# Attention with stacked rotary queries, pre-scaled queries and query projections between the heads

## The chip, the cores and the metric

The kernel runs on one core of one Trainium2 chip. The metric is the time of one execution in microseconds of device time. Engines are named as in the profile: PE is TensorE (PEld its weight loads), DVE is VectorE, ACT is ScalarE, POOL is GpSimd, SP is SyncE, which here only issues DMAs. Matrix products go from on-chip memory into eight PSUM banks of 128 x 512 float32; ACT and DVE read them from there.

## The reference

A two-layer trunk: layer 0 mixes tokens with an mLSTM, layer 1 with multi-head latent attention, and each is followed by a gated convolutional FFN and LayerNorms. 256 latent tokens attend to 256 context tokens and themselves. What the change touches is the attention of layer 1 (8 heads, 128 dimensions without and 64 with rotary position, values of 128):

```python
def _mla_q(h, w_dq, q_norm, w_uq, ang):
    q = (_rms_norm(h @ w_dq, q_norm) @ w_uq).reshape(B, T, A_HEADS, A_DNOPE + A_DROPE)
    q_nope, q_rope = jnp.split(q, [A_DNOPE], axis=-1)
    return jnp.concatenate([q_nope, _axial_rope(q_rope, ang[0][:, None], ang[1][:, None])], -1)

def _mla_kv(h, w_dkv, kv_norm, w_ukv, ang):
    ckv, k_rope = jnp.split(h @ w_dkv, [A_KVLORA], axis=-1)
    if ang is not None:
        k_rope = _axial_rope(k_rope, ang[0], ang[1])
    kv = (_rms_norm(ckv, kv_norm) @ w_ukv).reshape(B, T, A_HEADS, A_DNOPE + A_DV)
    k_nope, v = jnp.split(kv, [A_DNOPE], axis=-1)
    k = jnp.concatenate([k_nope, broadcast(k_rope over the heads)], -1)
    return k, v

def _attend(q, k, v):
    s = jnp.einsum("bqhd,bkhd->bhqk", q, k).astype(jnp.float32) * ((A_DNOPE + A_DROPE) ** -0.5)
    p = jax.nn.softmax(s, axis=-1).astype(v.dtype)
    return jnp.einsum("bhqk,bkhd->bqhd", p, v)
```

The rotary key is one for all heads. The result goes through `w_out`, then gate, residual and LayerNorm, then the FFN of layer 1.

## The kernel before

Numbers are float32, but matrix products run on a reduced type (float32r). Each operand is therefore split into a high part (a cast on ACT) and a low part (source minus high part, on DVE), and a product is three passes into one accumulator: high x high, high x low, low x high (`mm3`, L310 to L314). A split of a PSUM tile is `split` (L316 to L318); a weight of 128 x 1024 is split in `Stream._split` (ACT L256, DVE L257).

Weights come in one fixed order (`_plan`) through `Stream`. SP loads them into a ring of three `raw` buffers (L239); a load waits until the split that used its buffer three places before has ended. `use(key)` splits ahead of use, up to eight places and not past `self.limit`; `pump(n)` sets that limit to place n of the order and splits up to it. Split weights lie in three buffers `w`, and some ("wide" ones) in the large pool `u` of 31 buffers, as `wu`. Small tiles (`s2`) come from a pool of 13.

Background work is written as generators: `self.bg` holds them, `tick()` runs one step, `drain()` runs all the rest. The engines' order is set by a scheduler when the kernel is built, from the program's order and its own estimate of times; on the chip each engine runs its instructions in that order and waits on semaphores.

The attention of layer 1, in the order of the program:

- `mla_ctx`: the context's `dkv` product (512 context and latent columns share `ckT0`, `ckT1` and `krT`), root-mean-square norm, transposes (`dkv_T`). `krT` holds the rotary key transposed, copied twice, on rows 0 to 63 and 64 to 127; high part in index 0, low part in index 1.
- `mla_kv`, `ukn(0)`, `uv(0)`: keys and values of the context. Meanwhile `after0` ends the LayerNorm of the FFN before. A last piece of it, `ln_x`, is put off (`late`): four broadcast loads of gain and bias on POOL's queue (L932), then eight DVE operations (L1032, L1033) and four stores to `x2d` (L1034), which the residual of the attention reads later.
- `mla(hl)`: `dkv` and `dq` products of the latent tokens, norms, `dkv_T`, `ukn(1)`, transposes of the normed queries (`cqT`), `uv(1)` (24 passes into `v`), the rotary queries `qr` (weights `uqr`) with their rotation on DVE (`rope_rows`), then the other queries `qn` of all eight heads (weights `uqn`, with a `tick()` after each head, which is where the steps of `ln_x` are run), then the rotary queries transposed and split: `qrT` holds two heads per 128 rows, 64 rows each. `drain()` follows.
- The heads, a pipeline in which the scores of head h are followed by `attend` of head h - 2. `scores(h)`: per tile of 128 queries three passes of `qn` with `kn` on 128 rows and three of `qrT` with `krT` on 64 rows, row maximum (L1337), times minus the scale (L1338), exponential with scale, bias and sum (L1340), reciprocal and scaling (L1341, L1342). `trans`: eight transposes of P, split. `attend`: twelve passes with `v`, split into `oT`.
- `pump(ao + h)` stands ahead of heads 1 to 7; `ao` is the place of the first `aout` weight, so `aout` 0 to 6 are split in the heads.
- `aout`, the product with `w_out`: weight k belongs to head k, and `aout` 0 is used before the last head's `attend`. Then LayerNorm (`after0`: `ln_rows`, `ln_T`) while the first six `fin1` weights of the FFN are split, then the FFN.

Of the kernel before, what the change touches and what calls it, by code (L numbers as in the profile page):

```python
# [7 lines left out]
F32 = mybir.dt.float32  # L8
F32R = mybir.dt.float32r
I32 = mybir.dt.int32  # L10
AF = mybir.ActivationFunctionType
ALU = mybir.AluOpType
AX = mybir.AxisListType
# [12 lines left out]
H1 = 8  # L26
DN, DR, DV = 128, 64, 128
# [4 lines left out]
NB, NRAW, NU = 3, 3, 31  # L32
# [251 lines left out]
class K:  # L284
# [863 lines left out]
    def dkv_mm(self, hT, wd):  # L1148
        rows = [self.ps("dkv"), self.ps("dkv")]
        for k in range(8):  # L1150
            w = wd[k // 3]
            c = slice((k % 3) * 320, (k % 3 + 1) * 320)
            hi, lo = hT(k)
            for t in range(2):
                ts = slice(t * 128, (t + 1) * 128)
                self.mm3(rows[t][:, :320], (hi[:, ts], lo[:, ts]), (w[0][:, c], w[1][:, c]), k == 0, k == 7)
        return rows
# [17 lines left out]
    def dkv_T(self, out, t0):  # L1175

        nc = self.nc
        g = self.smc("kvg")
        cs = slice(t0 * 128, t0 * 128 + 256)
        for k in range(3):  # L1180
            pt = self.ps("ckT")
            for t in range(2):
                nc.tensor.transpose(pt[:, t * 128:(t + 1) * 128], out[t][:, k * 128:(k + 1) * 128], self.ident)
            p = pt[:, 0:256]
            if k < 2:
                u = self.ckT[k]
                nc.scalar.activation(u[:, 0, cs], p, AF.Copy, scale=g[:, k:k + 1])
                nc.vector.scalar_tensor_tensor(u[:, 1, cs], p, g[:, k:k + 1], u[:, 0, cs],
                                               op0=ALU.mult, op1=ALU.subtract)
            else:  # L1190
                self.split(self.krT[:, 0, cs], self.krT[:, 1, cs], p)

    def ukn(self, g):

# [26 lines left out]
    def mla_ctx(self, hc):  # L1221
        self.wd = [self.st.use(("dkv", 0, c), hold=True) for c in range(3)]
        self.ckT = [self.u("ckT0"), self.u("ckT1")]
        self.krT = self.u("krT")
        self.dkv_T(self.dkv_rows(self.dkv_mm(hc, self.wd), 0), 0)

    def rope_load(self):
# [13 lines left out]
    def mla(self, hl):  # L1241
# [2 lines left out]
        rows = self.dkv_rows(self.dkv_mm(hl, self.wd), 2)  # L1244
        self.wd = None
        st.unhold("dkv")
        pss = [self.ps("dq0"), self.ps("dq1")]
        for c in range(4):
            w = st.use(("dq", 0, c))
            for kk in range(2):  # L1250
                k = 2 * c + kk
                hi, lo = hl(k)
                cs = slice(kk * 384, (kk + 1) * 384)
                for t in range(2):
                    ts = slice(t * 128, (t + 1) * 128)
                    self.mm3(pss[t][:, :384], (hi[:, ts], lo[:, ts]), (w[0][:, cs], w[1][:, cs]), k == 0, k == 7)
# [9 lines left out]
        for k in range(3):  # L1266
# [5 lines left out]
            nc.vector.scalar_tensor_tensor(u[:, 1], pt[:, 0:256], g[:, k:k + 1], u[:, 0],  # L1272
                                           op0=ALU.mult, op1=ALU.subtract)
            cqT.append(u)
        self.uv(1)
        self.ckT = self.wk = self.wv = None
        kn, v = self.kn, self.v1
        pss = [self.ps("qr0"), self.ps("qr1")]
        for c in range(2):
            w = st.use(("uqr", 0, c))  # L1280
            for kk in range(2 - c):
                k = 2 * c + kk
                cs = slice(kk * 512, (kk + 1) * 512)
                for t in range(2):
                    ts = slice(t * 128, (t + 1) * 128)
                    self.mm3(pss[t], (cqT[k][:, 0, ts], cqT[k][:, 1, ts]), (w[0][:, cs], w[1][:, cs]),
                             k == 0, k == 2)
        qr = []
        for t in range(2):
            r = self.s2("qr")  # L1290
            self.rope_rows(r, pss[t], t, 512)
            qr.append(r)
        self.ropet = None
        qn = []
        ws = {}
        for h in range(H1):
            if h % 2 == 0:
                ps = self.ps("qn")
            hs = slice((h % 2) * 256, (h % 2 + 1) * 256)
            for k in range(3):  # L1300
                b = h * 3 + k
                if b % 8 == 0:
                    ws = st.use(("uqn", 0, b // 8))
                c = slice((b % 8) * 128, (b % 8 + 1) * 128)
                self.mm3(ps[:, hs], (ws[0][:, c], ws[1][:, c]), (cqT[k][:, 0], cqT[k][:, 1]), k == 0, k == 2)
            if h % 2:
                u = self.u("qn")
                self.split(u[:, 0], u[:, 1], ps)
                qn.append(u)
            self.tick()  # L1310
        qrT = []
        for i in range(2):
            pt = self.ps("qrT")
            for j in range(2):
                b = 2 * i + j
                for t in range(2):
                    nc.tensor.transpose(pt[:, j * 256 + t * 128:j * 256 + (t + 1) * 128],
                                        qr[t][:, b * 128:(b + 1) * 128], self.ident)
            u = self.u("qrT")
            self.split(u[:, 0], u[:, 1], pt)  # L1320
            qrT.append(u)
        self.drain()
        scale = float((DN + DR) ** -0.5)
        krT = self.krT

        def scores(h):
            Ps = []
            for t in range(2):
                ps = self.ps("s1")
                c = slice((h % 2) * 256 + t * 128, (h % 2) * 256 + (t + 1) * 128)  # L1330
                self.mm3(ps, (qn[h // 2][:, 0, c], qn[h // 2][:, 1, c]), (kn[h][:, 0], kn[h][:, 1]), True, False)
                b = h // 2
                r = slice((h % 2) * 64, (h % 2 + 1) * 64)
                c = slice((b % 2) * 256 + t * 128, (b % 2) * 256 + (t + 1) * 128)
                self.mm3(ps, (qrT[b // 2][r, 0, c], qrT[b // 2][r, 1, c]), (krT[r, 0], krT[r, 1]), False, True)
                mx, sm = self.tiny(1, "mx"), self.tiny(1, "sm1")
                nc.vector.tensor_reduce(mx, ps, axis=AX.X, op=ALU.max)  # L1337
                nc.vector.tensor_scalar(mx, mx, -scale, None, op0=ALU.mult)  # L1338
                P = self.s2("P1")
                nc.scalar.activation(P, ps, AF.Exp, bias=mx, scale=scale, accum_out=sm)  # L1340
                nc.vector.reciprocal(sm, sm)  # L1341
                nc.vector.tensor_scalar(P, P, sm, None, op0=ALU.mult)  # L1342
                Ps.append(P)
            return Ps
# [29 lines left out]

        ao = st.nu
        Ps, PTs = {}, {}
        for h in range(H1 + 1):
            if 1 <= h < H1:
                st.pump(ao + h)
            if h >= 2:  # L1380
                PTs[h - 2] = trans(h - 2, Ps.pop(h - 2))
            if h < H1:
                Ps[h] = scores(h)
            if h >= 2:
                attend(h - 2, PTs.pop(h - 2))
        yield oT
# [179 lines left out]
```

## Time and profile before

| | us |
|---|---|
| median of 3 runs (lowest, highest) | 1441.57 (1440.91, 1443.89) |
| the profiled execution | 1443.13 |
| its span, from the first to the last instruction | 1441.4 |
| PE busy in it | 1408.5 (98%) |
| DVE busy | 981.0 (68%) |
| ACT busy | 639.7 (44%) |
| POOL busy | 100.0 (7%) |
| mean granted clock of TensorE | 0.991 |

Durations and starts below are from the profiled execution, in microseconds from the start of its span. [...] The granted clock is the share of full speed that TensorE was given. The attention of layer 1 lies between about 1075 (the context's `dkv`) and 1240 (the end of `aout`), its heads between 1159.6 and 1217. A wait is put down to what came last before it ended.

### The profile page before, as it was taken

Reading aid. Unit: us, or ns where it says so; the run is one execution under the profiler, and the core shown is the slowest. Engines: PE = TensorE matmul, PEld = TensorE weight load, DVE = VectorE, ACT = ScalarE, POOL = GpSimd, SP = SyncE. Lnnn points to the kernel's source line nnn. Section 1 sums busy time; section 2 is a strip of 40 time slices with the busy share of each in tenths; the row PEclk is TensorE's granted clock in tenths of the full one; section 3 lists DMA queues with packets and bytes.
Section 4 is the critical chain, followed back from the end, with each engine's and each line's share of the span. In section 5 each row is a group of like instructions: output and inputs, shape, how many; then the busy total and the mean of one; then the engine's idle time right before and its main releaser. Section 6 shows DMA issues by size and latency. Waiting matters only on the chain.

```text
span 1441.4 us, 18835 instructions
## 1 busy us (share of the span) xinstructions
PE 1408.5 (98%) x7094; PEld 1178.2 (82%) x7094; DVE 981.0 (68%) x1451; ACT 639.7 (44%) x968; POOL 100.0 (7%) x185
## 2 busy tenths in 40 slices
PE   7999999999999999999999999999999989999997
PEld 3788888888878888878888888888888967899986
DVE  6796879985676676666787544444658677777756
ACT  6554232224333354464643333334455545555542
POOL 0011010003001010210001000000000001000000
PEclk9999999999999999999999999999999989999999
DMA  9475776777774645645645333345564334357763
GB/s 338 167 237 193 241 249 208 257 237 275 238 225 152 203 162 160 192 174 171 213 129 174 89 116 123 119 124 181 184 187 145 126 108 133 135 177 214 226 202 103
DMA packets 82828, 262.71 MB, mean 182 GB/s; under 512 B 11352, under 2 KB 19752, under 8 KB 82736
## 3 DMA queue, kind: packets, MB, share of 16 engines
q1 hardware_dynamic: 68304, 214.82, 46.6%
q0 software_dynamic: 14144, 46.17, 9.4%
q8 instruction: 55, 0.90, 0.3%
q10 hardware_dynamic: 288, 0.52, 0.1%
q14 instruction: 37, 0.30, 0.1%
HBM read 243.56 MB, written 17.91 MB: 181 GB/s over the span
## 4 chain that ended last, share of the span: by engine, by line
PE 67%; issue 18%; DMA 6%; DVE 4%; ACT 2%; POOL 2%; SPq 0%; DVEq 0%; POOLq 0%; ACTq 0%
PE fin L314 8%; PE fin L312 8%; PE fin L313 8%; PE y L313 5%; PE y L314 5%; PE y L312 5%; PE qk L312 4%; PE qk L314 4%; PE qk L313 4%; DMA raw<-in_ws 3%; DMA ar<-in_ada_w 2%; PE up L312 1%; PE up L314 1%; PE up L313 1%; PE s L312 1%
## 5 line engine op out<-in xcount | busy, mean ns | idle before, releaser
L257 DVE TENSOR_TENSOR w<-raw,w 128x1024 fp32r<-128x1024 f32 (+2 forms) x267 | 324.0, 1213 | 242.7 <-ACT w L256 242.1
L256 ACT CAST w<-raw 128x1024 fp32r<-128x1024 f32 (+2 forms) x267 | 278.8, 1045 | 437.3 <-PE tok L314 149.5
L314 PE MATMUL fin<-h,w 128*128 128x256 f32 (+1 forms) x696 | 231.6, 333 | 0.5 <-DVE w L257 0.5
L313 PE MATMUL fin<-h,w 128*128 128x256 f32 (+1 forms) x696 | 231.7, 333 | 0.0
L312 PE MATMUL fin<-h,w 128*128 128x256 f32 (+1 forms) x696 | 231.5, 334 | 0.0
L437 DVE SCALAR_TENSOR_TENSOR acc<-ar,cond,acc 128x1024 f32<-128x1024 f32 x112 | 140.6, 1279 | 36.2 <-DMA ar<-in_ada_w 35.9
L314 PEld LDWEIGHTS fin<-h,w 128*128 128x128 f32 x696 | 132.2, 190 | 13.8 <-DVE w L257 0.9
L313 PEld LDWEIGHTS fin<-h,w 128*128 128x128 f32 x696 | 132.2, 190 | 13.0 <-DVE h L1017 0.2
L312 PEld LDWEIGHTS fin<-h,w 128*128 128x128 f32 x696 | 131.9, 190 | 12.8
L314 PE MATMUL qk<-xc,w 128*128 128x512 f32 x256 | 100.2, 391 | 2.0 <-DVE w L257 2.0
L312 PE MATMUL qk<-xc,w 128*128 128x512 f32 x256 | 101.1, 395 | 0.0
L312 PE MATMUL tok<-w,xm 128*128 128x512 f32 x256 | 100.4, 392 | 0.0
L313 PE MATMUL qk<-xc,w 128*128 128x512 f32 x256 | 99.9, 390 | 0.0
L314 PE MATMUL tok<-w,xm 128*128 128x512 f32 x256 | 99.7, 389 | 0.0
L313 PE MATMUL tok<-w,xm 128*128 128x512 f32 x256 | 99.6, 389 | 0.0
L312 PE MATMUL y<-w,act 128*128 128x512 f32 (+1 forms) x212 | 80.4, 379 | 0.0
L313 PE MATMUL y<-w,act 128*128 128x512 f32 (+1 forms) x212 | 80.1, 378 | 0.0
L314 PE MATMUL y<-w,act 128*128 128x512 f32 (+1 forms) x212 | 80.1, 378 | 0.0
L314 PEld LDWEIGHTS qk<-xc,w 128*128 128x128 f32 x256 | 48.1, 188 | 12.7 <-DVE w L257 2.7
L312 PEld LDWEIGHTS tok<-w,xm 128*128 128x128 f32 x256 | 48.0, 188 | 10.3
L257 DVE TENSOR_TENSOR wu<-raw,wu 128x1024 fp32r<-128x1024 f32 x36 | 43.9, 1222 | 18.4 <-ACT wu L256 18.0
L314 PEld LDWEIGHTS tok<-w,xm 128*128 128x128 f32 x256 | 48.1, 188 | 10.1
(357 smaller groups left out, 2771.7 us busy)
## 6 DMA issues: line engine op xcount, KB each, us to landing
raw<-in_ws SPq DMA_DIRECT2D x300, 512.0 KB, 3.8
ar<-in_ada_w SPq DMA_DIRECT2D x80, 512.0 KB, 4.6
adaw<-in_ada_w SPq DMA_DIRECT2D x32, 256.0 KB, 6.0
xcd<-cv POOLq DMA_DIRECT2D x16, 256.0 KB, 3.3
od<-o POOLq DMA_DIRECT2D x16, 256.0 KB, 4.0
vd<-v POOLq DMA_DIRECT2D x16, 256.0 KB, 4.0
xcr<-xcd POOLq DMA_DIRECT2D x16, 256.0 KB, 6.3
vr<-vd POOLq DMA_DIRECT2D x16, 256.0 KB, 4.1
```

Source lines behind the costliest of these rows:

```text
L256: k.nc.scalar.copy(h[:, :cols], raw[:, :cols])
L257: k.nc.vector.tensor_sub(l[:, :cols], raw[:, :cols], h[:, :cols])
L312: mm(out, w[0], x[0], start=start, stop=False)
L313: mm(out, w[0], x[1], start=False, stop=False)
L314: mm(out, w[1], x[0], start=False, stop=stop)
L437: nc.vector.scalar_tensor_tensor(acc[j], w, s, acc[j], op0=ALU.mult, op1=ALU.add)
```

## The change

Five things change.

1. The rotary queries are split before they are transposed: `qrs` holds, per head, 64 high and 64 low columns, already times the scale. Transposed, one head fills 128 rows, the high part on rows 0 to 63 and the low part below. `krT` is the high key on both halves in index 0, and in index 1 the low key on rows 0 to 63 and zeros below (a memset in `mla_ctx`). Two passes then give the same three products: (high and low) x high, high x low. There are four transposed tiles instead of two, each with four transposes and one copy on ACT, and they lie in the pool `s2`.
2. The scale is put into the queries `qn` and `qrs` (`activation` with a scale, `scalar_tensor_tensor`), so the row maximum is negated by the reduction itself, L1338 goes, and the exponential has scale 1.
3. The queries of heads 0 to 3 and the first rotary pair are made ahead of the heads; those of heads 4 to 7 and the other rotary pairs between the heads.
4. `uv(1)` moves behind the `qr` product.
5. The steps of `ln_x` are run by new `tick()`s in `dkv_mm` and among the `dq` weights; the `drain()` stands behind the `qr` product.

`ao = st.nu` keeps its line, ahead of the heads; the three `uqn` weights are now used after it.

```diff
@@ -1151,6 +1151,7 @@
             w = wd[k // 3]
             c = slice((k % 3) * 320, (k % 3 + 1) * 320)
             hi, lo = hT(k)
+            self.tick(k % 2)
             for t in range(2):
                 ts = slice(t * 128, (t + 1) * 128)
                 self.mm3(rows[t][:, :320], (hi[:, ts], lo[:, ts]), (w[0][:, c], w[1][:, c]), k == 0, k == 7)
@@ -1188,7 +1189,8 @@
                 nc.vector.scalar_tensor_tensor(u[:, 1, cs], p, g[:, k:k + 1], u[:, 0, cs],
                                                op0=ALU.mult, op1=ALU.subtract)
             else:
-                self.split(self.krT[:, 0, cs], self.krT[:, 1, cs], p)
+                nc.scalar.copy(self.krT[:, 0, cs], p)
+                nc.vector.tensor_sub(self.krT[0:64, 1, cs], p[0:64], self.krT[0:64, 0, cs])
 
     def ukn(self, g):
 
@@ -1221,7 +1223,9 @@
     def mla_ctx(self, hc):
         self.wd = [self.st.use(("dkv", 0, c), hold=True) for c in range(3)]
         self.ckT = [self.u("ckT0"), self.u("ckT1")]
+
         self.krT = self.u("krT")
+        self.nc.vector.memset(self.krT[64:128, 1].bitcast(F32), 0.0)
         self.dkv_T(self.dkv_rows(self.dkv_mm(hc, self.wd), 0), 0)
 
     def rope_load(self):
@@ -1244,9 +1248,11 @@
         rows = self.dkv_rows(self.dkv_mm(hl, self.wd), 2)
         self.wd = None
         st.unhold("dkv")
+        self.tick()
         pss = [self.ps("dq0"), self.ps("dq1")]
         for c in range(4):
             w = st.use(("dq", 0, c))
+            self.tick()
             for kk in range(2):
                 k = 2 * c + kk
                 hi, lo = hl(k)
@@ -1272,9 +1278,6 @@
             nc.vector.scalar_tensor_tensor(u[:, 1], pt[:, 0:256], g[:, k:k + 1], u[:, 0],
                                            op0=ALU.mult, op1=ALU.subtract)
             cqT.append(u)
-        self.uv(1)
-        self.ckT = self.wk = self.wv = None
-        kn, v = self.kn, self.v1
         pss = [self.ps("qr0"), self.ps("qr1")]
         for c in range(2):
             w = st.use(("uqr", 0, c))
@@ -1285,42 +1288,53 @@
                     ts = slice(t * 128, (t + 1) * 128)
                     self.mm3(pss[t], (cqT[k][:, 0, ts], cqT[k][:, 1, ts]), (w[0][:, cs], w[1][:, cs]),
                              k == 0, k == 2)
+        self.drain()
+        self.uv(1)
+        self.ckT = self.wk = self.wv = None
+        kn, v = self.kn, self.v1
+        scale = float((DN + DR) ** -0.5)
+
         qr = []
         for t in range(2):
             r = self.s2("qr")
             self.rope_rows(r, pss[t], t, 512)
-            qr.append(r)
+            u = self.pool.tile([128, H1, 2, 64], F32R, tag="u", name="qrs", bufs=NU)
+            v3 = r.rearrange("p (h f) -> p h f", h=H1)
+            nc.scalar.activation(u[:, :, 0], v3, AF.Copy, scale=scale)
+            nc.vector.scalar_tensor_tensor(u[:, :, 1], v3, scale, u[:, :, 0], op0=ALU.mult, op1=ALU.subtract)
+            qr.append(u)
         self.ropet = None
-        qn = []
-        ws = {}
-        for h in range(H1):
-            if h % 2 == 0:
-                ps = self.ps("qn")
-            hs = slice((h % 2) * 256, (h % 2 + 1) * 256)
-            for k in range(3):
-                b = h * 3 + k
-                if b % 8 == 0:
-                    ws = st.use(("uqn", 0, b // 8))
-                c = slice((b % 8) * 128, (b % 8 + 1) * 128)
-                self.mm3(ps[:, hs], (ws[0][:, c], ws[1][:, c]), (cqT[k][:, 0], cqT[k][:, 1]), k == 0, k == 2)
-            if h % 2:
-                u = self.u("qn")
-                self.split(u[:, 0], u[:, 1], ps)
-                qn.append(u)
-            self.tick()
-        qrT = []
-        for i in range(2):
+        qn, qrT = [], []
+        wq = {}
+
+        def queries(i):
+
+            ps = self.ps("qn")
+            for h in (2 * i, 2 * i + 1):
+                hs = slice((h % 2) * 256, (h % 2 + 1) * 256)
+                for k in range(3):
+                    b = h * 3 + k
+                    if b % 8 == 0:
+                        wq[0] = st.use(("uqn", 0, b // 8))
+                    c = slice((b % 8) * 128, (b % 8 + 1) * 128)
+                    self.mm3(ps[:, hs], (wq[0][0][:, c], wq[0][1][:, c]), (cqT[k][:, 0], cqT[k][:, 1]),
+                             k == 0, k == 2)
+            u = self.u("qn")
+            nc.scalar.activation(u[:, 0], ps, AF.Copy, scale=scale)
+            nc.vector.scalar_tensor_tensor(u[:, 1], ps, scale, u[:, 0], op0=ALU.mult, op1=ALU.subtract)
+            qn.append(u)
+
+        def rotary(i):
+
             pt = self.ps("qrT")
             for j in range(2):
-                b = 2 * i + j
                 for t in range(2):
                     nc.tensor.transpose(pt[:, j * 256 + t * 128:j * 256 + (t + 1) * 128],
-                                        qr[t][:, b * 128:(b + 1) * 128], self.ident)
-            u = self.u("qrT")
-            self.split(u[:, 0], u[:, 1], pt)
+                                        qr[t][:, 2 * i + j].rearrange("p a b -> p (a b)").bitcast(F32), self.ident)
+            u = self.pool.tile([128, 512], F32R, tag="s2", name="qrT", bufs=13)
+            nc.scalar.copy(u, pt)
             qrT.append(u)
-        self.drain()
-        scale = float((DN + DR) ** -0.5)
+
         krT = self.krT
 
         def scores(h):
@@ -1329,15 +1343,12 @@
                 ps = self.ps("s1")
                 c = slice((h % 2) * 256 + t * 128, (h % 2) * 256 + (t + 1) * 128)
                 self.mm3(ps, (qn[h // 2][:, 0, c], qn[h // 2][:, 1, c]), (kn[h][:, 0], kn[h][:, 1]), True, False)
-                b = h // 2
-                r = slice((h % 2) * 64, (h % 2 + 1) * 64)
-                c = slice((b % 2) * 256 + t * 128, (b % 2) * 256 + (t + 1) * 128)
-                self.mm3(ps, (qrT[b // 2][r, 0, c], qrT[b // 2][r, 1, c]), (krT[r, 0], krT[r, 1]), False, True)
+                for x in range(2):
+                    nc.tensor.matmul(ps, qrT[h // 2][:, c], krT[:, x], start=False, stop=x == 1)
                 mx, sm = self.tiny(1, "mx"), self.tiny(1, "sm1")
-                nc.vector.tensor_reduce(mx, ps, axis=AX.X, op=ALU.max)
-                nc.vector.tensor_scalar(mx, mx, -scale, None, op0=ALU.mult)
+                nc.vector.tensor_reduce(mx, ps, axis=AX.X, op=ALU.max, negate=True)
                 P = self.s2("P1")
-                nc.scalar.activation(P, ps, AF.Exp, bias=mx, scale=scale, accum_out=sm)
+                nc.scalar.activation(P, ps, AF.Exp, bias=mx, scale=1.0, accum_out=sm)
                 nc.vector.reciprocal(sm, sm)
                 nc.vector.tensor_scalar(P, P, sm, None, op0=ALU.mult)
                 Ps.append(P)
@@ -1374,6 +1385,9 @@
 
         ao = st.nu
         Ps, PTs = {}, {}
+        queries(0)
+        queries(1)
+        rotary(0)
         for h in range(H1 + 1):
             if 1 <= h < H1:
                 st.pump(ao + h)
@@ -1381,6 +1395,10 @@
                 PTs[h - 2] = trans(h - 2, Ps.pop(h - 2))
             if h < H1:
                 Ps[h] = scores(h)
+            if h < 6 and h % 2 == 1:
+                rotary(h // 2 + 1)
+            if h < 2:
+                queries(h + 2)
             if h >= 2:
                 attend(h - 2, PTs.pop(h - 2))
         yield oT
```

## The prediction

> **What bounds the kernel now.** I read three views. First, the busy time of each engine in stretches of the trace, around the attention of layer 1 (columns: stretch in us, length, busy us and instructions of each engine, granted clock of TensorE, DMA share, GB/s).
>
> ```profile
> core 0: us, PE busy (x) PEld busy (x) DVE busy (x) ACT busy (x) POOL busy (x), PEclk, DMA share, GB/s
> 1166.40:1171.10 4.70, 0.01 (x1) 0.04 (x1) 4.61 (x12) 2.28 (x6) 0.00 (x0) 0.84 0.48 142
> 1171.10:1183.30 12.20, 12.20 (x39) 9.05 (x40) 6.56 (x18) 4.60 (x12) 0.00 (x0) 0.50 0.09 33
> 1183.30:1217.15 33.85, 33.85 (x189) 25.10 (x189) 27.26 (x63) 19.47 (x43) 3.83 (x7) 1.00 0.41 132
> 1217.15:1239.90 22.75, 22.71 (x131) 19.51 (x129) 19.02 (x28) 12.65 (x15) 1.63 (x3) 1.00 0.68 219
> 1239.90:1244.50 4.60, 1.54 (x13) 1.31 (x13) 2.80 (x9) 2.49 (x6) 0.00 (x0) 1.00 0.04 12
> ```
>
> TensorE (PE) is busy nearly everywhere, so what counts is what PE must do and where it pauses. There are two pauses: 1166.4 to 1171.1, with DVE busy 4.61 of 4.70 us, after which PE runs 12.2 us at a granted clock of 0.50; and the LayerNorm after `aout` (1239.9 to 1244.5), after which the clock stays at 1.00. Second, the chain that ended last, through the first pause (start, us, what):
>
> ```profile
> 1165.74 0.69 DVE mx L1337
> ...
> 1167.63 1.13 DVE wu L257
> 1168.76 0.61 DVE mx L1337
> ...
> 1171.09 2.06 PE PT L1355 x8
> ```
>
> The first pause is DVE's: the scores are done at 1165.7, but the row maxima (L1337) share DVE's queue with two weight splits (L257), and PE gets the first softmax only at 1171.09. DVE is late because from 1155.6 to 1164.1 it worked off the query splits, the eight `ln_x` operations (L1032, L1033; four pairs of 1.28 to 1.29 us, 5.1 us) and the two `qrT` splits. Third, PE's instructions in one head at full clock (start, us, engine, line, operation, shapes):
>
> ```profile
> 1195.60 0.40 PE L314 MATMUL s<-kn,qn 128*128 128x512 f32 x1
> 1195.92 0.49 PE L312 MATMUL s<-krT,qrT 64*128 64x512 f32 x1
> 1196.26 0.39 PE L313 MATMUL s<-krT,qrT 64*128 64x512 f32 x1
> 1196.49 0.39 PE L314 MATMUL s<-krT,qrT 64*128 64x512 f32 x1
> 1196.81 0.50 PE L312 MATMUL s<-kn,qn 128*128 128x512 f32 x1
> ```
>
> Three passes on 128 rows alternate with three on 64 rows. Inside a group matmuls start 0.23 us apart; across each change of row count, and for the one after it, 0.32 to 0.34. One head's twelve take 3.53 us (1189.20 to 1192.73), and a head's whole period on PE is 5.86 us (its transposes start at 1188.41, the next one's at 1194.27): 0.79 transposes, 3.53 scores, 1.54 `attend`. In the groups of instructions (1159 to 1217; line, engine, operation, shapes, count, busy and mean ns, idle before), DVE's share of a head:
>
> ```profile
> L1337 DVE TENSOR_REDUCE mx<-s 128x1 f32<-128x512 f32 x16 | 10.9, 682 | 5.1 <-PE s L314 5.1
> ...
> L318 DVE TENSOR_TENSOR PT<-PT,PT 128x512 fp32r<-128x512 f32 x14 | 9.3, 681 | 1.2 <-ACT PT L317 1.2
> ...
> L257 DVE TENSOR_TENSOR wu<-raw,wu 128x1024 fp32r<-128x1024 f32 x6 | 7.3, 1220 | 0.8 <-ACT wu L256 0.8
> ```
>
> **The change, part by part.** Its sum is made against the profiled execution, 1443.13 us with a span of 1441.4 and 1.7 around it; that is 1.6 above the median of 1441.57, so I subtract the sum from the median.
>
> *The pause goes: +10.8 us.* PE loses 4.7 idle plus half of the 12.2 cold, 6.1. In the built order of the changed kernel the eight `ln_x` operations stand on DVE before and around the splits of `dq`, rope and `qr` splits run under the 24 `v` matmuls (5.45 us, as 1140.6 to 1146.1 shows), and only two query pairs precede the first head. DVE then reaches the first maximum just as the scores end. The cover on PE is 18 query matmuls, ten score matmuls, four transposes and 18 more query matmuls before the first transposes of P: 2.14 + 2.30 + 0.44 + 2.14 = 7.0 us, against maximum 0.68, exponential 0.88, reciprocal 0.15 and scaling 0.48, some 3.2 for two tiles. Without this cover the pause is back.
>
> *Scores in five full-row passes: +10.7.* Ten matmuls at 0.23 make 2.30; `attend` loses its row change (1.43, twelve at 0.119). 0.79 + 2.30 + 1.43 = 4.52 against 5.86, 1.34 for each of eight heads. The trace has no such rotary pass. Lower bound: only a pass saved per tile, 16 x 0.23 = 3.7, if the cost of 0.1 belongs to the tile change and not the rows. I take 10.7, since the `s<-kn,qn` rows with 128 rows run at 0.23.
>
> *Eight more `qrT` transposes: -0.9* (eight take 0.87 at 1159.00). Two `qr` splits with strided output (DVE 0.68 as L318's 128x512; at worst twice, 1.4, under the `v` matmuls), four copies for two `qrT` splits on ACT, a memset of half a tile (0 to 0.7) and 16 fewer `mx` scalings (0.15) end no wait as long as PE leads.
>
> *DVE becomes nearly the bound: -2.6.* Per head DVE needs two maxima 1.20, two reciprocals 0.24, two scalings 0.80, two P splits 1.20 and one oT split 0.34 (by their starts back to back): 3.78, and 4.92 with a weight split of 1.14. PE needs 4.52. By the built order three heads carry a split (3 x 0.4 = 1.2), the fourth rotary copy stands behind two P casts and an exponential on ACT (0.5), and the last `attend`s wait for late low halves (0.9). Bounds: 0, and 7.8 if every head takes 5.5.
>
> *`ln_x` earlier: -0.5.* Two operations fit DVE's idle 1.93 us before 1114.8; the other six (3.6 us) end about when `dq`'s first low half is needed (1124.2). The four broadcasts on POOL's queue now wait for tiles freed before 1095, so nothing is behind them; the x2d stores go early. Bounds 0 to 2.
>
> *The pump is counted from an earlier place: -3.3.* `ao = st.nu` is now read before the three `uqn` are used, so `pump(ao + h)` ends three weights earlier: aout 0 to 3 instead of 0 to 6 are split in the heads, and aout 4 to 6 fall into the stretch from the last transposes on (1217.15 to 1239.9). There DVE is busy 19.0 of 22.75 us; three more splits (3.4) leave no slack. SP's loads keep their order, but each waits for a split three places before, so aout 7 is issued only some 3.8 us after the last transposes, lands after 4.2 (median here) and is split at 10.3; PE has passes of the next output tile before it in the built order, so it loses little. But two splits for `fin1` now stand between the last tile's first LayerNorm operation and its statistics (2.3), and the queue before them is 1.0 late. Bounds 0 (the 3.7 us of DVE slack takes it) and 6.
>
> *The second pause cools the clock: -4.5.* PE's idle 2.67 us before 1242.54 grows to about 6. 2.67 left the clock at 1.00, 4.72 lowered it, so I take it as lowered. Price: 12.2 us at half from 1171.1, or 6.0 at the kernel's start (matmuls resume at 16.79, granted 0.50 until 22.8): 6.1 or 3.0, middle 4.5; 0 if it holds.
>
> [...]
>
> Sum: 10.8 + 10.7 - 0.9 - 2.6 - 0.5 - 3.3 - 4.5 = 9.7; 1441.6 - 9.7 = **1432 us** (profiled execution: 1433.4).
>
> **The rivals.**
> - *The LayerNorm gap leaves the clock alone:* 14.2 gained, 1427.4. For it: 2.67 was harmless, and 6 is my own walk; against: 4.72 was not.
> - *DVE sets the pace of all heads* (5.5 us each: 4.92 and 0.6 of waiting for casts): 7.8 instead of 2.6, 1437. For it: DVE is already busy 27.3 of 33.9 us after 1183; against: only three heads carry a weight split.
> [...]
> - *The pause stays* (the change does not do what it says: DVE is still late for the first maximum): 10.8 less, 1442.7.
> - *Slower: weights late after the heads.* Loads are issued only as splits free their three buffers. Landing at 7.4 us (the longest `raw` load) instead of 4.2, a round of load, cast 1.0 and split 1.15 takes 9.6 us for three weights; then fin1's sixth split comes about 12 us later than the LayerNorm's old end, and PE goes cold twice (12): 24 against 17.5 gained, 1448. It decides from landings of about 6 us on; loads in this stretch took 4.4 with DMA share 0.68, which speaks against it.
>
> **How the numbers follow.** Chances: forecast 0.46, clock kept 0.26, DVE's pace 0.12, clock soon back 0.05, pause stays 0.06, weights late 0.05. A difference under 0.2% (2.9 us) can't be told from none here. Faster by more: 0.46 + 0.26 + 0.05 and most of 0.12, 0.87; within: 0.08; slower: 0.05. Range 1425 to 1439: down to clock kept with a cheaper pump, up to DVE's pace; it leaves out the last two cases.
>
> **What would show it.** No idle time of PE over 1 us and a clock of 1.00 from the first scores to the last; score matmuls 0.23 apart, no 64-row forms; head periods of 4.5 to 5.0; the last head's transposes some 17.5 us earlier; only three `wu` splits inside the heads, four `aout` splits behind them; a longer `zT` wait after `aout` with a granted clock of 0.50 behind it. I am wrong if PE still waits for P at the first head, if 128-row rotary passes are 0.3 apart, or if the gap after `aout` stays under 3 us.

## The result and the profile after

The changed kernel takes 1433.76 us (median of 6 runs, 1430.30 to 1435.37); the kernel before, measured beside it, 1441.76 (6 runs, 1439.50 to 1444.43). The medians are 8.0 us apart; the ratio is 0.9937 with a 95% interval of 0.9922 to 0.9952, which is 9.1 us, 6.9 to 11.2. The profiled execution took 1434.82 us with a span of 1433.0, against 1443.13 and 1441.4.

First, the busy time of each engine in stretches of the changed kernel's trace, with limits at its own events (columns as before: stretch in us, length, busy us and instructions of each engine, granted clock of TensorE, DMA share, GB/s).

```profile
core 0: us, PE busy (x) PEld busy (x) DVE busy (x) ACT busy (x) POOL busy (x), PEclk, DMA share, GB/s
1153.30:1158.00 4.70, 4.70 (x41) 4.67 (x40) 4.63 (x8) 3.44 (x6) 0.00 (x0) 1.00 0.00 2
1158.00:1167.49 9.49, 9.49 (x63) 8.44 (x62) 7.30 (x15) 6.39 (x13) 0.00 (x0) 1.00 0.36 113
1167.49:1202.20 34.71, 34.20 (x225) 30.66 (x224) 29.78 (x61) 22.66 (x51) 3.91 (x7) 1.00 0.30 99
1202.20:1227.18 24.98, 23.25 (x131) 19.43 (x129) 18.86 (x27) 14.09 (x17) 1.63 (x3) 1.00 0.65 208
1227.18:1232.19 5.01, 0.00 (x1) 0.01 (x1) 4.51 (x10) 2.10 (x4) 0.00 (x0) 0.67 0.56 183
1232.19:1235.70 3.51, 3.51 (x17) 3.51 (x17) 1.94 (x5) 2.93 (x8) 0.00 (x0) 0.50 0.42 135
```

The first three lines are the stretch ahead of the scores, the first two heads' scores with the queries of later heads between them, and the heads from the first transposes of P (1167.49) to the last head's (1202.20). The pause ahead of the first P is gone: PE is busy 4.70 of 4.70 and 9.49 of 9.49 us, and the clock is 1.00 to the last head. The last three lines are the new cost. Behind `aout` PE stands still for 5.01 us (2.67 before), and the 3.51 us of work behind that run at a granted clock of 0.50, called half clock below.

Second, PE's instructions in one head of the changed kernel (start, us, engine, line, operation, shapes):

```profile
1168.28 0.47 PE L312 MATMUL s<-kn,qn 128*128 128x512 f32 x1
1168.60 0.39 PE L313 MATMUL s<-kn,qn 128*128 128x512 f32 x1
1168.83 0.40 PE L314 MATMUL s<-kn,qn 128*128 128x512 f32 x1
1169.06 0.62 PE L1347 MATMUL s<-krT,qrT 128*128 128x512 f32 x2
1169.52 0.39 PE L312 MATMUL s<-kn,qn 128*128 128x512 f32 x1
```

Each tile has three passes for the queries and two for the rotary part, all on 128 rows and 0.23 us apart (0.32 for the first behind the transposes); there is no 64-row form left. One is listed with 0.39 us or more and the next starts before it ends, so what one costs in a row is told by the distance between starts. Third, DVE's share of the heads (groups of instructions, 1153 to 1202.2):

```profile
L1349 DVE TENSOR_REDUCE mx<-s 128x1 f32<-128x512 f32 x16 | 10.9, 684 | 1.4 <-PE s L1347 1.3
L318 DVE TENSOR_TENSOR PT<-PT,PT 128x512 fp32r<-128x512 f32 x14 | 9.1, 680 | 0.2 <-ACT PT L317 0.2
...
L257 DVE TENSOR_TENSOR wu<-raw,wu 128x1024 fp32r<-128x1024 f32 x3 | 3.7, 1218 | 0.2 <-ACT wu L256 0.2
```

In the heads `wu` is split three times, where the groups of before (1159 to 1217) have six. Fourth, DVE in the time in which PE waits behind `aout` (start, us, engine, line, operation):

```profile
1227.24 0.41 DVE L946 TENSOR_TENSOR z<-y,gate 128x256 f32<-128x256 f32 x1
1227.65 1.23 DVE L257 TENSOR_TENSOR w<-raw,w 128x1024 fp32r<-128x1024 f32 x1
1228.79 0.42 DVE L947 SCALAR_TENSOR_TENSOR z<-xres,z 128x256 f32<-128x256 f32 x1
1229.13 1.22 DVE L257 TENSOR_TENSOR w<-raw,w 128x1024 fp32r<-128x1024 f32 x1
1230.26 0.42 DVE L949 BATCH_NORM_STATS2 st<-z 128x6 f32<-128x256 f32 x1
...
1231.59 0.54 DVE L977 TENSOR_SCALAR z<-z,mv,rs 128x512 f32<-128x512 f32 x1
```

Two weight splits of 1.23 and 1.22 us (L257) stand between the last operations on `z` (1227.24, 1228.79) and its statistics (1230.26). The last operation on `z` starts at 1231.59 and takes 0.54; PE starts at 1232.19.

Where the time went in the two profiled executions, in four stretches. The limits are the last `cqT` transposes (1140.55 before, 1143.67 after), the last head's transposes (1217.15, 1202.20), the end of `fin1`, taken as the start of its last matmul (1371.19, 1361.84), and the end of the span:

| stretch | before | after | gain |
|---|---|---|---|
| start to `cqT` | 1140.55 | 1143.67 | -3.12 |
| `cqT` to the last head's transposes | 76.60 | 58.53 | +18.07 |
| from there to the end of `fin1` | 154.04 | 159.64 | -5.60 |
| end of `fin1` to the end | 70.17 | 71.13 | -0.96 |
| sum | 1441.36 | 1432.97 | +8.39 |

Of the first line, 2.20 us are there before any changed instruction has run: the first `dkv` matmul starts at 1077.33 before and at 1079.53 after. Fourteen traces of this study have it between 1075.17 and 1079.64, with the same code ahead of it. The last stretch, which no variant touches either, lies between 70.1 and 71.3. So 3.2 us of difference in this pair are the chance of two executions, and the changed code gained 11.55 in it (-0.92 + 18.07 - 5.60). With the mean of four traces of before in place of one (they follow below) it is -1.10 + 16.32 - 5.06 = 10.2, inside the interval of the runs, in its upper half.

### The profile page after: what moved, and what is told of

Same layout as the page of the kernel before. It is cut to its first block, busy times and chain, and to the rows that moved or that the text cites. A ratio compares the mean times of both kernels' runs of the same rounds, so it can differ in the third digit from the quotient of the medians.

```text
span 1433.0 us, 18800 instructions
## 1 busy us (share of the span) xinstructions
PE 1398.2 (98%) x7086; PEld 1176.4 (82%) x7086; DVE 979.7 (68%) x1436; ACT 641.8 (45%) x972; POOL 100.1 (7%) x185
## 4 chain that ended last, share of the span: by engine, by line
PE 64%; issue 18%; DVE 6%; DMA 6%; ACT 3%; POOL 2%; DVEq 0%; SPq 0%; POOLq 0%; ACTq 0%
PE fin L314 8%; PE fin L313 8%; PE fin L312 8%; PE y L313 5%; PE y L314 5%; PE y L312 5%; PE qk L314 4%; PE qk L312 4%; PE qk L313 4%; DMA raw<-in_ws 3%; DMA ar<-in_ada_w 2%; PE adar L402 1%; PE up L312 1%; DVE wu L257 1%; PE up L313 1%
## 5 line engine op out<-in xcount | busy, mean ns | idle before, releaser
L257 DVE TENSOR_TENSOR w<-raw,w 128x1024 fp32r<-128x1024 f32 (+2 forms) x267 | 323.9, 1213 | 240.5 <-ACT w L256 240.0
L257 DVE TENSOR_TENSOR wu<-raw,wu 128x1024 fp32r<-128x1024 f32 x36 | 43.9, 1222 | 24.3 <-ACT wu L256 23.8
```

The costliest lines, as they stand in the source:

```text
L257: k.nc.vector.tensor_sub(l[:, :cols], raw[:, :cols], h[:, :cols])
```

## The experiments

Times are medians; "trace" is the stretch from the last `cqT` transposes to the last head's transposes, 58.53 in the changed kernel, which is free of what happens ahead of it. Each kernel was timed beside the kernel before, so the ratios are the safest comparison between kernels; the medians of the kernel before alone differ by 1.0 us.

| kernel | us | ratio to before (95%) | trace, us |
|---|---|---|---|
| before (four traces) | 1441.8 to 1442.7 | 1 | 72.65 to 76.85 |
| changed | 1433.76 | 0.9937 (0.9922 to 0.9952) | 58.53 |
| a_pump | 1428.83 | 0.9906 (0.9891 to 0.9922) | 59.88 |
| a_lnx_late | 1438.45 | 0.9971 (0.9960 to 0.9982) | 65.22 |
| a_ahead | 1433.88 | 0.9940 (0.9925 to 0.9955) | 60.26 |
| b_stack | 1435.79 | 0.9957 (0.9942 to 0.9972) | 66.28 |
| a_three | 1441.55 | 0.9989 (0.9978 to 1.0001) | 67.90 |
| a_uv | 1435.32 | 0.9948 (0.9930 to 0.9966) | 62.93 |
| a_scale | 1437.14 | 0.9954 (0.9937 to 0.9971) | 60.60 |
| p_act | 1425.91 | 0.9882 (0.9866 to 0.9899) | 59.14 |
| l_three | 1439.81 | 0.9974 (0.9958 to 0.9991) | 67.52 |

**a_pump: the pump counted from its old place.**

```diff
-        ao = st.nu
+        ao = st.nu + 3
```

> The changed kernel with the pump counted from where it was counted before: ao = st.nu + 3 instead of ao = st.nu, nothing else. Theory (counting from the earlier place leaves weight splits for the time after the heads, they make the LayerNorm after aout late, and its wait of 5.01 us costs 6.8 us of half clock, 3.5 of them with work on TensorE): five or six splits of aout weights stand before the last head's transposes instead of three, the heads become up to 1.2 us longer, the wait for z after aout falls to about 2.7 us, no half clock behind it; in all 3 to 5 us faster than the changed kernel, 1429 to 1431 us. Rival (DVE is the bound from the heads to the LayerNorm, so that it does not matter where its splits stand): the heads become longer by about 3.4 us, the z wait and the clock stay as they are or the gain there is eaten by the heads; 1433 to 1435 us.

1428.83 us, 4.9 less than the changed kernel. Stretches of its trace:

```profile
1166.35:1202.39 36.04, 34.58 (x225) 30.50 (x224) 32.15 (x64) 24.96 (x54) 3.85 (x7) 1.00 0.44 139
...
1225.38:1227.98 2.60, 0.00 (x1) 0.01 (x1) 2.04 (x7) 0.78 (x2) 0.00 (x0) 1.00 0.00 2
1227.98:1231.40 3.42, 3.00 (x24) 2.76 (x25) 2.23 (x6) 3.17 (x9) 0.00 (x0) 1.00 0.00 0
```

Six `wu` splits stand in the heads, and these take 36.04 us instead of 34.71. The wait behind `aout` is 2.60, with the clock at 1.00 behind it; from the last head's transposes to the end of `fin1` it takes 154.24 instead of 159.64. So 5.4 come back and 1.35 are paid in the heads: the theory, and the rival falls. The place at which `st.nu` is read, one line that the change leaves as it was, costs 4.9 us by the medians (4.5 by the ratios) where the whole change gains 8.0 (9.1).

**a_lnx_late: the three new ticks taken out.**

```diff
             hi, lo = hT(k)
-            self.tick(k % 2)
...
         st.unhold("dkv")
-        self.tick()
...
             w = st.use(("dq", 0, c))
-            self.tick()
```

> The changed kernel without the three new ticks, so that all eight ln_x operations run at the drain, behind the qr matmuls. Theory (the pause before the first P is gone because queries of later heads cover it, and the early ln_x is worth only the time it blocks): DVE has 5.1 us more to do between the qr matmuls and the qr splits, 2.3 of it in idle time, so the first rotary transposes come about 1 us later; the first P had 4.4 us of slack, so no pause over 2.7 us and a clock of 1.00 through the heads; the stage up to the qr matmuls gets back up to 0.9 us; in all within 1.5 us of the changed kernel, 1432 to 1435 us. Rival (it is the early ln_x that took the pause away): PE waits 3 us or more at the first rotary transposes or at the first P and the clock halves behind it; 1437 to 1444 us.

1438.45 us, 4.7 slower. By time and by the length of its waits, the rival is right (l_three below narrows what that means): PE waits for the split rotary queries, then for the queries' copy (PE by start; in brackets the idle time before it and who ended it), and the clock halves behind that:

```profile
1159.27 0.33 PE L1329 MATMUL qrT<-ident,qrs 128*128 128x128 f32 x1 [2.03 <-DVE qrs L1301]
1161.02 0.79 PE L312 MATMUL s<-kn,qn 128*128 128x512 f32 x1 [1.42 <-ACT qn L1320]
```

```profile
1161.02:1167.23 6.21, 6.21 (x19) 5.14 (x20) 3.11 (x6) 3.08 (x5) 0.00 (x0) 0.50 0.37 126
```

2.03 + 1.42 us idle, and half of the 6.21 at 0.50, 3.1: 6.55 of the 6.69 by which its trace is longer. I had given the first rotary transposes 1 us of delay. It was 2, and the splits of the query pair stand behind the rotary splits on ACT and DVE, which I had left out. At the first P, where the kernel before pauses, PE does not wait here.

**a_ahead: all queries and rotary tiles ahead of the heads.**

```diff
         queries(1)
-        rotary(0)
+        queries(2)
+        queries(3)
+        for i in range(4):
+            rotary(i)
...
-            if h < 6 and h % 2 == 1:
-                rotary(h // 2 + 1)
-            if h < 2:
-                queries(h + 2)
```

> The changed kernel with all four pairs of queries and all four rotary tiles computed ahead of the heads, none between them. Theory (covers): between the first scores and the first transposes of P only the second head's scores (2.3 us) are left; P was ready 2.5 us after its scores, later with two maxima in between, so PE waits 0.5 to 2 us at the first P, less than the 2.67 us that left the clock at 1.00; 0.5 to 2 us slower than the changed kernel, 1434 to 1436 us. Rival 1 (the interleaving is what removed the pause): PE waits over 3.4 us, the clock halves; 1438 to 1443 us. Rival 2 (the early ln_x alone was enough): no wait, 1433 to 1434 us.

1433.88 us, the changed kernel's time within the interval. Its only wait up to the first transposes of P:

```profile
1166.61 0.44 PE L1366 MATMUL PT<-ident,P 128*128 128x128 f32 x2 [1.18 <-DVE P L1353]
```

1.18 us, and the clock stays at 1.00: the theory. Its trace stretch is 1.73 longer, which the runs cannot tell from nothing. With the early `ln_x`, the queries between the heads cover little more than a microsecond.

**b_stack: the stacked rotary queries alone, in the kernel before.** Two passes, strided splits of `qr`, four `qrT` tiles, the zeroed half of `krT`; order, pump, ticks and scale as before.

```diff
-                self.mm3(ps, (qrT[b // 2][r, 0, c], qrT[b // 2][r, 1, c]), (krT[r, 0], krT[r, 1]), False, True)
+                for x in range(2):
+                    nc.tensor.matmul(ps, qrT[h // 2][:, c], krT[:, x], start=False, stop=x == 1)
```

> The kernel before with one part of the change alone: high and low rotary queries stacked in 128 rows and two passes instead of three of 64 rows. Order, pump, ln_x and the scale stay as before. Theory (a change of row count costs 0.1 us at each matmul beside it, besides the pass itself): a head's scores take 2.3 us instead of 3.53, 9 to 10 us gained in the heads less 0.9 of transposes and some 2 of waiting for DVE; the pause before the first P stays at about 4.7 us and the clock halves behind it. If 64-row passes count as less work for the clock, the half clock now lasts 6.8 us or less instead of 13.65 and 3 us more are gained: 1430 to 1432 us; if they do not, it lasts 13.65 us again: 1433 to 1435 us. Rival (only the pass itself is saved, 0.23 for each of 16 tiles): 1438 to 1440 us.

1435.79 us, 6.9 less than before. Its first pause and what follows:

```profile
1165.17:1169.23 4.06, 0.01 (x1) 0.03 (x1) 3.96 (x11) 2.21 (x6) 0.00 (x0) 0.97 0.57 145
1169.23:1172.39 3.16, 3.16 (x12) 2.72 (x13) 2.70 (x9) 1.86 (x6) 0.00 (x0) 0.50 0.38 148
1172.39:1206.71 34.32, 33.23 (x205) 28.30 (x204) 30.83 (x74) 21.84 (x48) 3.99 (x7) 1.00 0.41 130
```

The pause is there (4.06), but only 3.16 us run at half clock behind it, where the trace shown of before had 12.2. The heads from there on take 34.32 us with PE busy 33.23: DVE has five weight splits in them besides its 3.78 a head. With the half clock this short the theory had said 1430 to 1432, so it missed by about 4: the passes gave less than 9 to 10. That DVE then sets the pace of more heads is the likely reason, but it is argued and not shown.

**a_three: the changed kernel with three 64-row passes.** `qr`, `qrT`, `krT` and the passes as before, with the scale in the `qrT` split.

> The changed kernel with the three passes of 64 rows put back (queries not stacked, two qrT tiles of two parts), all else as changed. Theory (the row change costs 0.1 us at each matmul beside it): a head's scores take 3.5 us again and its period 5.8, so DVE is hidden; 9.3 to 10.7 us lost in the heads, 0.9 of transposes and about 1 of waiting for DVE and ACT regained: 1440 to 1443 us. Rival 1 (only the pass itself, 16 x 0.23 us): 1436 to 1437 us. Rival 2 (in this order DVE sets the pace of the heads, so that TensorE's passes are nearly free): 1434 to 1436 us.

1441.55 us, 7.8 slower: the theory. Its heads are 5.86 us apart on PE (transposes at 1169.00, 1174.86, 1180.72), as before; the trace stretch is 9.37 longer. Both rivals fall: beside a change of rows a matmul of before takes 0.32 or 0.34 us, and with full rows 0.23, and DVE does not set the pace of the changed kernel's heads as a whole.

**a_uv: uv(1) back ahead of the `qr` matmuls.**

```diff
+        self.uv(1)
+        self.ckT = self.wk = self.wv = None
         pss = [self.ps("qr0"), self.ps("qr1")]
...
         self.drain()
-        self.uv(1)
-        self.ckT = self.wk = self.wv = None
```

> The changed kernel with uv(1) (24 v matmuls, 5.4 us) back ahead of the qr matmuls. Theory (the v matmuls cover rope and the qr splits on DVE): after the qr matmuls PE has two pairs of queries, 4.3 us, and DVE some 5 us of rope and splits and one or two weight splits of 1.2, so the first rotary transposes wait 2 to 3 us; whether the clock halves behind it depends on how much of the wait falls into one 3.41 us stretch; 1436 to 1440 us. Rival (DVE leads here since the v splits are done before the qr matmuls end): wait under 1 us, 1434 us.

1435.32 us, 1.6 slower, just below the theory's range and above the rival. PE waits twice, 2.48 in all, and 3.41 us run at half clock:

```profile
1154.23 0.33 PE L1332 MATMUL qrT<-ident,qrs 128*128 128x128 f32 x1 [1.06 <-DVE qrs L1304]
1155.98 0.50 PE L312 MATMUL s<-kn,qn 128*128 128x512 f32 x1 [1.42 <-ACT qn L1323]
```

So 4.2 of the 4.4 by which its trace stretch is longer. The interval of the runs does not part it from the changed kernel.

**p_act: on top of a_pump, P of every second token tile scaled on ACT.**

```diff
-                nc.vector.tensor_scalar(P, P, sm, None, op0=ALU.mult)
+                if t:
+                    nc.scalar.activation(P, P, AF.Copy, scale=sm)
+                else:
+                    nc.vector.tensor_scalar(P, P, sm, None, op0=ALU.mult)
```

> The kernel with the pump counted from its old place, and in it the scaling of P of every second token tile on ACT instead of DVE. Theory (DVE sets the pace of those heads that carry a weight split: periods of 5.0 where TensorE needs 4.5): DVE loses 0.4 us a head, 8 x 0.4 = 3.2, the heads become 1 to 2 us shorter; 1427 to 1428 us. Rival (ACT's queue is the bound: the scaling waits for exponential, accumulator and reciprocal, and the P casts stand behind it): heads as long or longer, 1429 to 1432 us.

1425.91 us, the lowest of the study, 1.2% less than before. The heads in its trace:

```profile
1163.04:1198.35 35.31, 34.85 (x226) 30.70 (x225) 30.21 (x58) 28.67 (x61) 3.84 (x7) 1.00 0.46 142
```

35.31 us against 36.04 in a_pump, with DVE busy 30.2 instead of 32.2: 0.7 gained, where 1 to 2 were expected. The other 2.2 between the medians lie outside what was changed, and the intervals overlap; that it beats both given kernels is shown, that it beats a_pump is not.

**l_three: three 64-row passes and no new ticks.**

> The changed kernel without the three new ticks and with three passes of 64 rows. It asks what sets the length of a half-clock stretch. [...] Without a pause nothing is told of the clock; then 1440 to 1443 us.

1439.81 us, just under the 1440 to 1443. There is no pause ahead of the heads at all, so it tells nothing of the clock. But it differs from a_three by the three ticks alone, and it is no slower without them (0.9974 against 0.9989, the intervals overlap). So in the changed order a late `ln_x` by itself brings no pause. It suggests why a_lnx_late pauses: with 64-row passes the rotary transposes take the rope's result as it is; with stacked queries they wait for the two `qr` splits, which stand behind `ln_x` on DVE.

**b_again, b_third, b_fourth: the kernel before three times more**, one trace each.

> The kernel before once more, for a second trace of its two pauses. Theory (TensorE's clock is decided by stretches of 3.41 us, and a stretch with 1.5 us of 64-row passes in it does not bring it back): the half clock behind the first P lasts 10.2 or 13.65 us again, over two stretches without a gap on TensorE, wherever the limits of the stretches fall; with the same pause the kernel with five full-row passes had 3.41. Rival (the 13.65 was chance): 3.41 or 6.83. The parts of the trace ahead of the first dkv matmul, which no variant touches, end between 1075 and 1080 us.

> The kernel before, a third trace, to tell whether the length of the half clock behind the first P hangs on where the 3.41 us stretches fall. Theory (a stretch with idle time or with 64-row passes in it does not bring the clock back, one of full-row work does): if the first stretch behind the first P holds less than 0.3 us of idle time and less than 0.3 us of 64-row passes, 3.41 us of half clock; if it holds more idle time, the following ones hold 64-row scores and the half clock lasts 10.2 or 13.65 us. Rival (64-row passes do not matter): the first stretch without a gap ends the half clock, 3.41 or 6.83 us.

> The kernel before, a fourth trace, for the same question and by the same numbers as the third: 3.41 us of half clock where the first stretch behind the first P is full of 128-row work, 10.2 or 13.65 us where it begins with idle time; rival: 3.41 or 6.83 us in either case.

1442.97, 1442.18 and 1444.19 us. The pause is 4.71 to 4.72 in all of them; the work at half clock behind it is not the same (first line b_again, then b_third, then b_fourth):

```profile
1173.26:1176.59 3.33, 3.33 (x12) 2.43 (x12) 2.88 (x9) 1.80 (x5) 0.00 (x0) 0.50 0.32 119
```

```profile
1172.00:1176.60 4.60, 4.60 (x14) 3.16 (x14) 3.34 (x9) 1.77 (x5) 0.00 (x0) 0.50 0.25 95
```

```profile
1171.73:1184.37 12.64, 12.64 (x41) 9.50 (x42) 6.89 (x19) 5.03 (x12) 0.00 (x0) 0.50 0.08 30
```

3.33, 4.6 and 12.64 us, after 12.2 in the first trace. For b_again I had expected 10 us or more, and for b_third too where the first 3.41 us behind P hold idle time (they held 2.20): both missed, and the rival's 3.41 and 6.83 came. b_fourth (1.01 of idle time) came as the theory said. Half of these is what the clock costs: 1.7, 2.3, 6.3 and 6.1 us in four executions of one kernel.

**a_scale: the scale back in the softmax**, with 16 more scalings of `mx` on DVE and plain splits of `qrs` and `qn`. The lines of the softmax:

```diff
-                nc.vector.tensor_reduce(mx, ps, axis=AX.X, op=ALU.max, negate=True)
+                nc.vector.tensor_reduce(mx, ps, axis=AX.X, op=ALU.max)
+                nc.vector.tensor_scalar(mx, mx, -scale, None, op0=ALU.mult)
...
-                nc.scalar.activation(P, ps, AF.Exp, bias=mx, scale=1.0, accum_out=sm)
+                nc.scalar.activation(P, ps, AF.Exp, bias=mx, scale=scale, accum_out=sm)
```

> The changed kernel with the scale back in the softmax: plain splits of queries and rotary queries, and 16 more mx scalings on DVE (0.15 us each). Theory (0.3 us of DVE a head counts only in the three heads that carry a weight split and at the first P, which has 4 us of slack): 0 to 1 us slower than the changed kernel, 1433 to 1435 us. Rival (each scaling stands between the maximum and the exponential and delays every P): 2.4 us and more, 1436 to 1438 us.

1437.14 us, 3.4 slower, with an interval that reaches the changed kernel's; the trace stretch is 2.07 longer. The rival is nearer. One head late in the row shows it (PE, then ACT):

```profile
1194.60 0.87 PE L1365 MATMUL PT<-ident,P 128*128 128x128 f32 x6 [1.29 <-DVE P L1352]
```

```profile
1192.59 0.69 ACT L1350 ACTIVATE P<-s,mx 128x512 f32<-128x512 f32 x1 [1.59 <-DVE mx L1348]
```

The transposes wait 1.29 us for P there, and never over 0.36 in the changed kernel's heads. ACT's exponential had waited 1.59 us for the scaling of `mx`: the maximum was done at 1191.38, but three other operations stood between it and its scaling (1192.35) in DVE's queue. The small operation is on the way from the maximum to P, and what it costs is its place in a full queue, not its 0.15 us.

## Why the prediction was right, step by step

The forecast was 9.7 us; the medians say 8.0 (interval of the ratio 6.9 to 11.2). The single terms were less good than their sum.

- **The pause goes, 10.8.** It went: no idle time of PE over 0.36 us between the last `cqT` transposes and the last head's, clock 1.00. Of the price, 4.7 of idle time is the same in four traces. The 6.1 of half clock was one draw of four (1.7 to 6.3, mean 4.1), so a size off by about 2.
- **"Without this cover the pause is back."** This step failed. Without the queries between the heads (a_ahead) PE waits 1.18 us at the first P, not 4.7, and the clock stays. Without the early `ln_x` PE does not wait at the first P either: a_lnx_late pauses ahead of it, at the rotary transposes and the first scores (3.45 idle and 3.1 of clock), and l_three not at all. So either of the two keeps the old pause small. The early `ln_x` and uv(1) behind `qr` (a_uv: 2.48 and 1.7) guard against a new pause: in both kernels PE first waits for `qrs`, the split of the stacked queries. No run takes the cover and the early `ln_x` out together; b_stack, with all of the old order, has the old pause (4.06).
- **Five full-row passes, 10.7, and eight transposes, -0.9.** Right: a_three loses 9.37 in its stretch. A head's scores take 2.38 (0.77, 0.46, 0.69, 0.46 from start to start), not 2.30.
- **DVE nearly the bound, -2.6.** Too large. The heads from 1167.49 to 1202.20 have seven times eight transposes (5.5), six heads' scores (14.3), seven `attend` (10.0), eight `qrT` transposes (0.7) and 15 `aout` matmuls (3.5), 34.0 of 34.71: 0.7 waited. Together, these four terms gave 18.0 against a measured 18.07, but that is the chance of one draw: against the mean of the four traces of before it is 16.3.
- **The small edits that "end no wait as long as PE leads".** Wrong twice. The 16 `mx` scalings are worth 2.07 in a_scale's trace, since PE does not lead in every head. And stacking comes with some 1.0 of loss far ahead of the heads. In every kernel with stacked queries PE waits 1.04 or 1.05 us for `z` in the LayerNorm that ends layer 0; in those with 64-row passes there is no such wait. The changed kernel shows it (PE, then DVE):

```profile
1110.88 0.98 PE L1004 MATMUL zT<-ident,z 128*128 128x128 f32 x7 [1.04 <-DVE z L977]
```

```profile
1094.49 0.48 DVE L1228 MEMSET krT<- 64x512 f32 x1 [0.16 <-issue]
```

The memset stands on DVE ahead of that LayerNorm's operations, but `z` comes no later for it: the operation on `z` that PE waits for starts 30.3 to 31.1 us after the first `dkv` matmul in the kernels with the wait, and 30.7 to 31.1 in those without. What differs is PE's built order: before `z` is done PE runs 30 `kn` passes in the former, 36 and two `v` passes in the latter, and these had covered it. From the first `dkv` matmul to the last `cqT` transposes it takes 64.0 to 64.5 us in seven of the eight kernels with stacked queries (63.6 in a_uv) and 62.9 to 63.6 in the others (b_stack against the mean of before: 1.1 more; changed against a_three: 0.5). Which line of the stacking turned the order is not shown.
- **`ln_x` earlier, -0.5.** Within error: 64.14 with early, 64.49 with late `ln_x`; with 64-row passes 63.63 and 63.07.
- **The pump from an earlier place, -3.3.** Right in mechanism and near in size: the wait of PE grew from 2.67 to 5.01, with 0.73 more in two shorter waits for `z` and 0.99 for a weight; a_pump gets 5.4 back, of which 1.75 is clock, so 3.65.
- **The clock cools, -4.5.** It did, as said, but took 3.51 us of work at half, 1.75. Of the cases in the chances it was "clock soon back", at 0.05, that came. The error was to price it by 12.2 and 6.0, the only two stretches in the one trace at hand.

So about 2 us too much for the first pause, 0.6 for eight heads' scores, 0.35 for the pump and 1.0 forgotten in the LayerNorm of layer 0 stood against 1.9 and 2.75 of loss that did not come, for DVE and for the second pause: 10.4 in place of 9.7, near the 10.2 of the traces. That errors of both signs nearly cancelled is luck. Why the medians are 2 us nearer to each other than the traces' means is not shown; it is within the interval.

## What to carry to other kernels

When a loop is moved in the code, look at every counter that is read beside it: the pump's start, read three weights earlier, gave back five of the microseconds won. Before an idle time is credited to the part of a change that seems made for it, take that part out alone; here the interleaving was worth at most two microseconds and the quiet move of `ln_x` about five. Ask then what makes it worth that: with 64-row passes the same move gained nothing (a_three against l_three); it seems to pay only where the stacked queries' splits stand behind `ln_x`. And a stretch of half clock seen in one trace is one draw: price it from several traces, or as a range.

## What the runs showed of the hardware

Behind the pauses of the attention the half clock lasted 13.65 us in the first trace of before (1169.63 to 1183.29) and in b_fourth, 6.83 in the changed kernel (1228.88 to 1235.70), a_lnx_late and b_third, and 3.41 in b_again, b_stack and a_uv: one, two or four times 3.41. Within one trace the changes of clock also lie whole steps of 3.4133 us apart: at 15.93, 22.76, 1169.63 and 1183.29 in before (2, 336 and 4 steps), at 17.14, 23.97, 1228.88 and 1235.70 in the changed kernel (2, 353 and 2).

Counted in these steps, from a trace's own changes of clock and behind its first 30 us, TensorE's idle time in the step just ahead of a half clock was 3.27 us in before, 2.43 in the changed kernel, 2.52 and 2.17 in b_third, and 2.66 behind `aout` in b_again. Steps that held 1.44 and 1.65 behind `aout` in before, and 1.82 in b_fourth, were followed by a clock of 1.00. So a wait of about 2.6 us behind `aout` went both ways: the clock stayed at 1.00 in the first trace of before (2.67), in a_pump (2.60) and in b_fourth (2.51), and halved in b_again, b_third, b_stack and p_act (2.60 to 2.67). In before and in b_fourth the wait lay across the limit of two steps; in b_again all of it lay in one step, in b_third 2.17 of its 2.66.

Behind a pause the clock was back at 1.00 after the first step with little idle time in b_again (0.08 us), b_stack (0.25), a_lnx_late (none, after a step with 0.62), b_third (none, after one with 2.20) and the changed kernel (none, after one with 3.31). In the first trace of before and in b_fourth it was not: in each, two steps without idle time, which held 1.57 or 1.58 us of matmuls on 64 rows, were followed by 0.50, and a third, without such matmuls, by 1.00. In b_third a step with 1.35 us of them was followed by 1.00. At half clock the starts are 0.55 to 0.60 us apart at the row changes, against 0.43 inside a group (before, 1172.80 to 1179.09). No run varies rows or the distance of starts alone, so whether either has to do with it stays open. At the start of the kernel, too, a step with 0.31 us of idle time and no matmul on 64 rows was followed by 0.50 (changed kernel, 17.14 to 20.55); its first starts are 0.73 and 0.59 apart.

Beside a change of row count a matmul took 0.1 us more on PE: a head's rotary part is six matmuls at 0.32 or 0.34 and 0.23 in before and four at 0.23 in the changed kernel, and the query passes beside them lost their 0.1 too. The 0.1 is not peculiar to rows: the first query pass behind the transposes takes 0.32 with 128 rows on both sides (1168.28 in the changed kernel).
